# Two output blocks at a time from seven half products instead of eight, in the gate, silu and output projections of a two-layer trunk

## The chip, the core and the metric

The kernel runs on one core of a Trainium2 chip. TensorE multiplies, VectorE and ScalarE work on tiles in SBUF and PSUM, and the SyncE queue (SP in the profile) issues every transfer. The metric is the device time of one execution, in microseconds (us). A kernel is executed several times; the median of the runs is its time.

## The reference, cut to what matters

640 tokens (512 latent, 128 context) pass through two layers. Each layer normalises its input `x`, modulates it to `h` (1024 features), projects it with `w_in`, runs three mixers (attention, DeltaNet, gated MLP) and merges them:

```
h    = rms(x) * (1 + scale) + shift              # 640 x 1024
proj = h @ w_in                                  # among its columns: z_a, z_b, z_c (512 each), gl (3 x 1024)
br   = [o_a * silu(z_a), o_b * silu(z_b), o_c * silu(z_c)]
yb_n = br_n @ w_branch[n]                        # 512 -> 1024, n = 0, 1, 2
y    = sum_n sigmoid(gl_n) * yb_n                # gates
x    = x + gate * (y @ w_o)                      # 1024 -> 1024
```

The change touches the projections of `h` that give `z_a` and part of `gl`, and the product with `w_o`.

## The kernel before, in words

Activations lie transposed: a feature block is a tile of 128 partitions (features) by 640 columns (tokens), and `h` is eight such tiles. An output block is 128 output features by 640 tokens. `dense` computes one in two halves of 320 columns, each a PSUM accumulation over the eight feature blocks. To keep single precision, every operand is split into a high part (rounded to the fast 32-bit format) and a low part (the remainder), and `mm3` adds three products: high by high, high by low, low by high. So one output block takes 2 x 8 x 3 = 48 matmuls of 320 columns, two blocks 96.

A weight block of 1024 x 128 comes as two tiles of 128 x 512 in buffers tagged `raw` (three of them). `wsplit` makes `hi` by a ScalarE copy and `lo` by a VectorE subtraction (three buffers each), one pair for each 128 x 512 tile. `h` lies split in the tiles `hh0`..`hh7` and `hl0`..`hl7`, later in a layer `y` takes the same tiles.

In a layer the order of the program is: DeltaNet and MLP, attention, then `branch(2)`, `branch(1)`, `branch(0)`, then the output projection with `w_o`. In `branch(n)`, `silu_block` makes the four `z` blocks (only n = 0 and 1), which are multiplied with the mixer's output and split (tiles `qkv`). Then, for m = 0..7, a gate block comes from `h` (48 matmuls, a ScalarE tanh of each half into a `th` tile), a block of `w_branch` from the split mixer (24 matmuls), and VectorE multiplies and adds into `yacc[m]` (tile `ya`). In layer 0, `branch(0)` also runs pieces of the modulation of the next layer between its blocks (`mod_fill`, weights in `G` tiles). After the branches, `yacc` is split into `hh`/`hl`, and eight blocks of `w_o` follow; the old `x`, which each needs, comes back by a transfer into an `ld` tile. At the end of layer 0 every new `x` block is also spilled and squared for the next norm (`norm_add`).

The order of the instructions is not that of the program. All operations are recorded and then placed on the engines by a planner (`Recorder.plan`), which simulates them with estimated costs: of the operations whose inputs are ready, each engine takes the one that comes first in the program; those recorded under `rec.hp()` go before all others. Tiles of one tag get their buffers strictly in program order, so an operation can't start until all earlier tiles of its tag have had theirs. That is why blocks of the branches run already during attention (their tags are `raw`, `hi`, `lo`, `dn`), as work for TensorE between the steps of the softmax. PSUM has two buffers of one bank (`dn`), two of one bank (`mm`) and two of two banks (tag `p2`, called p in the profile), which attention uses for its scores. The numbers of buffers that matter here: `G` 13, `V` 3, `qkv` 8, `C` 5, `D` 6, `iv` 8, `raw`, `hi` and `lo` 3 each.

The loop of the output projection:

```
        for m in range(KM):
            wk = wsplit(a["w_o"][l, m, 0]) + wsplit(a["w_o"][l, m, 1])
            xo = X("ld", [P, NT])
            SY.dma_start(xo, xsrc[m])
...
            dense(wk, yh, yl, evac)
```

Of the kernel before, what the change touches and what calls it, by code (L numbers as in the profile page):

```python
# [8 lines left out]
F32R = mybir.dt.float32r  # L9
# [414 lines left out]
def trunk_kernel(ctx: ExitStack, tc: tile.TileContext, a, o, depth=DEPTH, dump=None):  # L424
# [10 lines left out]
    def T(shape, tag, dt=F32, bufs=None, pool=None):  # L435
        uid[0] += 1
        kw = {} if bufs is None else {"bufs": bufs}
        t = (pool or sb).tile(shape, dt, tag=tag, name=f"{tag}_{uid[0]}", **kw)
        return rec.tile(t, tag, pool is ps, shape, bufs or (2 if pool is lay or pool is None else 1))
# [7 lines left out]
    def p2():  # L447
        return T([P, 1024], "p2", pool=ps, bufs=2)

    def X(tag, shape, dt=F32):  # L450
        return T(shape, tag, dt, bufs=NB[tag])
# [61 lines left out]
    def wsplit(src, m=P):  # L513

        n = src.shape[1]
        w, hi, lo = wload(src), X("hi", [P, 512], F32R), X("lo", [P, 512], F32R)
        with rec.hp():
            split_w(w[:, 0:n], hi[:, 0:n], lo[:, 0:n])
        return [(hi[:, c : c + m], lo[:, c : c + m]) for c in range(0, n, m)]
# [16 lines left out]
    class Side:  # L536
# [16 lines left out]
        def finish(self, evacs):  # L553
            for (wk, m), ac, evac in zip(self.blocks, self.acc, evacs):
                with rec.hp():
                    for hf in range(2):
                        evac(ac[hf][0:m, 0:HF], hf * HF, hf * HF + HF)


    class Mod:  # L560
# [114 lines left out]
    def spill(t):  # L675
        uid[0] += 1
        d_ = dram.tile([P, NT], F32, tag=f"sp{uid[0]}", name=f"sp{uid[0]}")
        rec.tile(d_, f"sp{uid[0]}", False, [P, NT], 1)
        SY.dma_start(d_, t)
        return d_  # L680
# [18 lines left out]
    def layer(l, md, hh, hl, fill, side):  # L699
# [7 lines left out]
        def win(b, evac):  # L707
            dense(wsplit(a["w_in"][l, b, 0]) + wsplit(a["w_in"][l, b, 1]), hh, hl, evac)
# [387 lines left out]
        def silu_block(b, tag):  # L1096
            zt = X(tag, [P, NT])

            def evac(acc, c0, c1):
                th = tanh2(acc)  # L1100
                V.scalar_tensor_tensor(zt[:, c0:c1], th, 1.0, acc, ALU.add, ALU.mult)

            win(b, evac)
            return zt
# [87 lines left out]
        def mod_fill():  # L1192

            if fill:
                next(fill[0])
                left[0] = (left[0] + 1) % 4
                if left[0] == 0:
                    fill.pop(0)


        def branch(n, brs):
            bh, bl = [], []
            for q, f in enumerate(brs):
                if n == 0:
                    mod_fill()
                if n < 2:
                    u = X("ld", [P, NT])
                    SY.dma_start(u, f)
                    f = silu_block((B_ZA, B_ZB)[n] + q, "C")
                    V.tensor_tensor(f, f, u, ALU.mult)  # L1210
                hi, lo = split2(f)
                bh.append(hi)
                bl.append(lo)
            for m in range(KM):
                if n == 0:
                    mod_fill()
                ga = {}

                def ev1(acc, c0, c1):
                    ga[c0] = X("th", [P, HF])  # L1220
                    S.activation(ga[c0], acc, AF.Tanh, scale=0.5)

                win(B_GL + 8 * n + m, ev1)
                first = len(yacc) <= m
                if first:
                    yacc.append(T([P, NT], f"ya{m}", bufs=1))
                y = yacc[m]

                def ev2(acc, c0, c1):
                    if first:  # L1230
                        V.scalar_tensor_tensor(y[:, c0:c1], ga[c0], 1.0, acc, ALU.add, ALU.mult)
                    else:
                        V.scalar_tensor_tensor(ga[c0], ga[c0], 1.0, acc, ALU.add, ALU.mult)
                        V.tensor_tensor(y[:, c0:c1], y[:, c0:c1], ga[c0], ALU.add)

                dense(wsplit(a["w_branch"][l, n, m]), bh, bl, ev2)
# [273 lines left out]
        for k in range(KM):  # L1510
# [4 lines left out]
            yh.append(hi_)  # L1515
            yl.append(lo_)
        last = l == depth - 1
        for m in range(KM):
            wk = wsplit(a["w_o"][l, m, 0]) + wsplit(a["w_o"][l, m, 1])
            xo = X("ld", [P, NT])  # L1520
            SY.dma_start(xo, xsrc[m])
            xn = T([P, NT], f"ya{m}", bufs=1)

            def evac(acc, c0, c1):
                cuts = ((0, c1, 0),) if c0 == 0 else ((c0, NL, 0), (NL, c1, 1))
                for b0, b1, s in cuts:
                    V.scalar_tensor_tensor(xn[:, b0:b1], acc[:, b0 - c0 : b1 - c0], md.gate[:, m, s : s + 1], xo[:, b0:b1], ALU.mult, ALU.add)

            dense(wk, yh, yl, evac)
            if last:  # L1530
                SY.dma_start(o["y"][:, m, :], xn)
            else:
                xt[m] = xn
                xsrc[m] = spill(xn)
                sq = norm_add(m)
        return None if last else sq


# [137 lines left out]
```

## Time and profile before

| | |
|---|---|
| median of 3 runs | 1734.79 us (1727.08 to 1734.96) |
| the profiled execution | 1730.23 us, its span 1728.4 us |
| TensorE matmul busy, instructions | 1680.2 us, 13550 |
| VectorE busy, instructions | 1078.8 us, 3202 |
| ScalarE busy, instructions | 812.6 us, 2065 |
| mean granted TensorE clock | 0.991 of full speed |

The span runs from the first to the last instruction; the rest of the execution's own time, 1.8 us, lies around it. Busy time counts overlapping instructions of an engine once. Matmuls are pipelined, so their durations overlap, and the distance from start to start says what one costs in a dense row. All operations are recorded by one helper, so every row bears its line, L372, and the tiles' names tell the operations apart.

### The profile page before, as it was taken

What the parts mean: (1) busy time and instruction counts of PE and PEld (TensorE: products, weight loads), DVE (VectorE), ACT (ScalarE), POOL (GpSimd) and SP (SyncE); (2) the same over time, 40 slices, a digit from 0 to 9 for tenths busy, and PEclk for the clock granted to TensorE, in tenths of its full rate; (3) what the DMA queues carried; (4) which work ended last, traced back from release to release, by engine and by line L of the source; (5) the groups of instructions that cost most, each with busy time, mean ns of one, the idle gap of its engine ahead of it and who ended that gap; (6) DMA issues with size and microseconds to landing.
All of it is one profiled execution on the core that took longest, in us unless ns stands there. A gap on an engine that the chain in (4) does not pass through costs nothing.

```text
span 1728.4 us, 34853 instructions
## 1 busy us (share of the span) xinstructions
PE 1680.2 (97%) x13550; PEld 1574.2 (91%) x13550; DVE 1078.8 (62%) x3202; ACT 812.6 (47%) x2065; POOL 16.6 (1%) x100
## 2 busy tenths in 40 slices
PE   6999999999999999999999999899999999999999
PEld 4998988999889889999989989889989888999999
DVE  4898898565656653433568988975655666434353
ACT  3566664554545542222335666655544555423231
POOL 0000000000000000000000000000000000000000
PEclk9999999999999999999999999999999999999999
DMA  9311221221112242655432212112221122123234
GB/s 289 94 57 51 61 56 56 67 63 53 56 48 70 64 135 74 188 170 167 134 126 69 57 38 60 60 52 66 67 59 54 38 82 60 58 79 104 74 97 133
DMA packets 94612, 146.36 MB, mean 85 GB/s; under 512 B 14064, under 2 KB 38000, under 8 KB 94448
## 3 DMA queue, kind: packets, MB, share of 16 engines
q1 hardware_dynamic: 94448, 144.15, 27.6%
q8 instruction: 106, 1.74, 0.4%
q14 instruction: 58, 0.48, 0.1%
HBM read 132.28 MB, written 11.83 MB: 83 GB/s over the span
## 4 chain that ended last, share of the span: by engine, by line
PE 89%; DVE 5%; ACT 4%; issue 1%; DMA 1%; SPq 0%; DVEq 0%; ACTq 0%
PE dn L372 63%; PE p L372 14%; PE mm L372 12%; ACT iv L372 1%; DVE C L372 1%; ACT G L372 1%; DVE G L372 1%; DVE iv L372 1%; DVE lo L372 1%; ACT hi L372 1%; ACT C L372 0%; DMA ya<-in_xT 0%; DVE R L372 0%; DVE qkv L372 0%; DVE st L372 0%
## 5 line engine op out<-in xcount | busy, mean ns | idle before, releaser
L372 PE MATMUL dn<-hh,hi 128*128 128x320 f32 (+1 forms) x2176 | 687.2, 316 | 5.5 <-ACT hh L372 2.2
L372 PE MATMUL dn<-hh,lo 128*128 128x320 f32 (+1 forms) x2176 | 687.3, 316 | 0.0
L372 PE MATMUL dn<-hl,hi 128*128 128x320 f32 (+1 forms) x2176 | 686.0, 315 | 0.6 <-DVE hl L372 0.6
L372 PEld LDWEIGHTS dn<-hh,hi 128*128 128x128 f32 (+1 forms) x2176 | 409.1, 188 | 18.1 <-issue 4.8
L372 PEld LDWEIGHTS dn<-hl,hi 128*128 128x128 f32 (+1 forms) x2176 | 408.9, 188 | 4.5 <-issue 1.7
L372 PEld LDWEIGHTS dn<-hh,lo 128*128 128x128 f32 (+1 forms) x2176 | 409.2, 188 | 2.4 <-issue 0.7
L372 DVE TENSOR_TENSOR lo<-raw,hi 128x512 fp32r<-128x512 f32 (+1 forms) x322 | 221.7, 688 | 233.3 <-ACT hi L372 222.1
L372 ACT CAST hi<-raw 128x512 fp32r<-128x512 f32 (+1 forms) x322 | 199.3, 619 | 300.5 <-PE dn L372 281.7
L372 PE MATMUL dn<-qkv,hi 128*128 128x320 f32 x768 | 176.3, 313 | 0.0
L372 ACT ACTIVATE th<-dn 128x320 f32<-128x320 f32 x176 | 76.7, 436 | 129.3 <-PE dn L372 129.1
L372 PEld LDWEIGHTS dn<-qkv,hi 128*128 128x128 f32 x768 | 129.9, 189 | 1.0 <-issue 1.0
L372 PE MATMUL dn<-qkv,lo 128*128 128x320 f32 x384 | 119.6, 312 | 0.0
L372 DVE TENSOR_REDUCE mx<-p 128x1 f32<-128x640 f32 x64 | 52.7, 823 | 60.3 <-PE p L372 60.3
L372 ACT ACTIVATE V<-p,mx,scl 128x640 f32<-128x640 f32 x64 | 56.8, 887 | 66.4 <-DVE mx L372 59.2
L372 PEld LDWEIGHTS dn<-qkv,lo 128*128 128x128 f32 x384 | 72.4, 189 | 0.0
L372 DVE SCALAR_TENSOR_TENSOR th<-th,dn 128x320 f32<-128x320 f32 x96 | 46.7, 486 | 40.8 <-PE dn L372 35.7
L372 PEld LDWEIGHTS p<-iv,G 32*32 32x32 f32 (+2 forms) x608 | 35.0, 133 | 36.0 <-issue 33.8
L372 ACT COPY V<-p 128x640 f32<-128x640 f32 x64 | 44.6, 697 | 48.0 <-PE p L372 47.7
L372 PE MATMUL p<-G,G 128*128 128x512 f32 x128 | 65.8, 596 | 0.0
L372 PE MATMUL mm<-V,G 128*64 128x128 f32 (+1 forms) x672 | 60.8, 278 | 0.0
L372 DVE TENSOR_TENSOR iv<-iv,iv 128x150 f32<-128x150 f32 (+15 forms) x244 | 57.9, 238 | 1.9
L372 PEld LDWEIGHTS mm<-V,G 128*64 128x64 f32 (+1 forms) x672 | 50.2, 149 | 5.8 <-issue 5.7
(305 smaller groups left out, 2345.1 us busy)
## 6 DMA issues: line engine op xcount, KB each, us to landing
raw<-in_w_in SPq DMA_DIRECT2D x244, 256.0 KB, 2.6
G<-in_w_mod SPq DMA_DIRECT2D x96, 256.0 KB, 4.4
raw<-in_w_branch SPq DMA_DIRECT2D x48, 256.0 KB, 2.6
raw<-in_w_o SPq DMA_DIRECT2D x32, 256.0 KB, 2.6
ld<-sp SPq DMA_DIRECT2D x24, 320.0 KB, 3.2
G<-in_w_uq SPq DMA_DIRECT2D x16, 192.0 KB, 2.7
ya<-in_xT SPq DMA_DIRECT2D x8, 320.0 KB, 5.8
sp<-V SPq DMA_DIRECT2D x8, 320.0 KB, 2.2
```

The lines of the kernel that those rows point to most:

```text
L372: op.ins = getattr(getattr(nc, ENG[op.eng]), op.meth)(*op.args, **op.kw)
```

## The change

`two_blocks` computes two output blocks together. The two blocks' weights are cut along the 1024 input features into an upper and a lower half: a11, a12 for the first block and a21, a22 for the second (each one 128 x 512 tile). The input is cut the same way along features, and along its 640 columns into left and right halves: b11, b12, b21, b22. The eight products of halves are replaced by Winograd's seven, of sums of weights and sums of inputs, and the results are put together by additions:

- weights: s1 = a21 + a22, s2 = s1 - a11, a11 - a21, a12 - s2 (VectorE, 128 x 512 each), and each of the seven factors is split into high and low;
- inputs: t1 = b12 - b11, t2 = b22 - t1, t3 = b22 - b12, t4 = b21 - t2, made and split once by `half_sums`, for `h` in branch 1 and for `y` after the branches;
- results: one ScalarE copy and seven VectorE additions of 128 x 320, all of which read PSUM.

Each product is 4 feature blocks x 3 = 12 matmuls of 320 columns, so a pair takes 84 matmuls. The accumulators are the four banks of the two `p2` tiles. The sums t1, t2, t3 lie in `G` (nine tiles) and `V` (three); t4 is written over the right halves of the first four input tiles, so after that the plain input isn't whole any more. a21, a22, s1, s2 lie in `D`, the results in `iv`.

It is used for the four `z` blocks of branch 0 (two pairs), all gate blocks of branch 0 (four pairs), the gates m = 4..7 of branch 1 (two pairs), and the blocks m = 2..7 of `w_o` (three pairs), in both layers: 22 pairs in all. The other blocks stay as they were. The old `x` for the output projection is loaded into `qkv` tiles instead of `ld`.

```diff
--- before.py
+++ after.py
@@ -555,6 +555,97 @@
                 with rec.hp():
                     for hf in range(2):
                         evac(ac[hf][0:m, 0:HF], hf * HF, hf * HF + HF)
+    def half_sums(full, xh, xl):
+        L_, R_ = slice(0, HF), slice(HF, NT)
+        b, t1, t2, t3, late = [], [], [], [], []
+        for k in range(4):
+            x0, x1 = full(k), full(k + 4)
+            t = X("C", [P, NT])
+            V.tensor_tensor(t[:, L_], x0[:, R_], x0[:, L_], ALU.subtract)
+            V.tensor_tensor(t[:, R_], x1[:, R_], x0[:, R_], ALU.subtract)
+            V.tensor_tensor(x0[:, L_], x1[:, R_], t[:, L_], ALU.subtract)
+            t4 = X("iv", [P, HF])
+            V.tensor_tensor(t4, x1[:, L_], x0[:, L_], ALU.subtract)
+            hi, lo, two = X("G", [P, NT], F32R), X("V" if k < 3 else "G", [P, NT], F32R), X("G", [P, NT], F32R)
+            S.copy(hi, t)
+            V.tensor_tensor(lo, t, hi, ALU.subtract)
+            S.copy(two[:, L_], x0[:, L_])
+            V.tensor_tensor(two[:, R_], x0[:, L_], two[:, L_], ALU.subtract)
+            t1.append((hi[:, L_], lo[:, L_]))
+            t3.append((hi[:, R_], lo[:, R_]))
+            t2.append((two[:, L_], two[:, R_]))
+            late.append(t4)
+        def last():
+            for k in range(4):
+                S.copy(xh[k][:, R_], late[k])
+                V.tensor_tensor(xl[k][:, R_], late[k], xh[k][:, R_], ALU.subtract)
+            q = lambda k, c: (xh[k][:, c], xl[k][:, c])
+            return {"b11": [q(k, L_) for k in range(4)], "b21": [q(k + 4, L_) for k in range(4)], "b22": [q(k + 4, R_) for k in range(4)],
+                    "t1": t1, "t2": t2, "t3": t3, "t4": [q(k, R_) for k in range(4)]}
+        return last
+    def two_blocks(src, B, evac):
+        a11, a12 = wload(src[0]), wload(src[1])
+        a21, a22 = X("D", [P, 512]), X("D", [P, 512])
+        SY.dma_start(a21, src[2])
+        SY.dma_start(a22, src[3])
+        s1, s2 = X("D", [P, 512]), X("D", [P, 512])
+        ab, cd = p2(), p2()
+        qa_, qb_, qc_, qd_ = ab[:, 0:HF], ab[:, 512 : 512 + HF], cd[:, 0:HF], cd[:, 512 : 512 + HF]
+        def product(w, b, out):
+            hi, lo = X("hi", [P, 512], F32R), X("lo", [P, 512], F32R)
+            with rec.hp():
+                split_w(w, hi, lo)
+            for k, (bh, bl) in enumerate(B[b]):
+                c = slice(P * k, P * k + P)
+                mm3(out, hi[:, c], lo[:, c], bh, bl, k == 0, k == 3)
+        def plus(out, x, y):
+            with rec.hp():
+                V.tensor_tensor(out, x, y, ALU.add)
+        def minus(out, x, y):
+            with rec.hp():
+                V.tensor_tensor(out, x, y, ALU.subtract)
+        plus(s1, a21, a22)
+        minus(s2, s1, a11)
+        product(a11, "b11", qa_)
+        product(s2, "t2", qb_)
+        u, v, x, y = (X("iv", [P, HF]) for _ in range(4))
+        with rec.hp():
+            S.copy(u, qa_)
+        plus(v, qb_, u)
+        product(s1, "t1", qc_)
+        minus(a21, a11, a21)
+        plus(x, qc_, v)
+        product(a12, "b21", qa_)
+        plus(u, qa_, u)
+        minus(a12, a12, s2)
+        with rec.hp():
+            evac(0, u, 0, HF)
+        product(a21, "t3", qb_)
+        plus(y, qb_, x)
+        plus(v, qb_, v)
+        with rec.hp():
+            evac(1, y, HF, NT)
+        product(a22, "t4", qd_)
+        plus(v, qd_, v)
+        with rec.hp():
+            evac(1, v, 0, HF)
+        product(a12, "b22", qc_)
+        plus(x, qc_, x)
+        with rec.hp():
+            evac(0, x, HF, NT)
 
 
     class Mod:
@@ -1197,16 +1288,31 @@
                 if left[0] == 0:
                     fill.pop(0)
 
+        def h_sum(k):
+            x = X("C", [P, NT])
+            V.tensor_tensor(x, hh[k], hl[k], ALU.add)
+            return x
+        B = {}
 
         def branch(n, brs):
+            first2 = (0, 4, KM)[n]
             bh, bl = [], []
             for q, f in enumerate(brs):
                 if n == 0:
                     mod_fill()
+                if n == 0 and q % 2 == 0:
+                    zs = [X("C", [P, NT]) for _ in range(2)]
+                    def evz(i, acc, c0, c1):
+                        V.scalar_tensor_tensor(zs[i][:, c0:c1], tanh2(acc), 1.0, acc, ALU.add, ALU.mult)
+                    two_blocks([a["w_in"][l, B_ZA + q + i, half] for i in range(2) for half in range(2)], B, evz)
                 if n < 2:
                     u = X("ld", [P, NT])
                     SY.dma_start(u, f)
-                    f = silu_block((B_ZA, B_ZB)[n] + q, "C")
+                    f = silu_block(B_ZB + q, "C") if n else zs[q % 2]
                     V.tensor_tensor(f, f, u, ALU.mult)
                 hi, lo = split2(f)
                 bh.append(hi)
@@ -1214,13 +1320,26 @@
             for m in range(KM):
                 if n == 0:
                     mod_fill()
-                ga = {}
-
-                def ev1(acc, c0, c1):
-                    ga[c0] = X("th", [P, HF])
-                    S.activation(ga[c0], acc, AF.Tanh, scale=0.5)
-
-                win(B_GL + 8 * n + m, ev1)
+                if m >= first2:
+                    if m % 2 == 0:
+                        if not B:
+                            B.update(half_sums(h_sum, hh, hl)())
+                        gates = {}
+                        def ev0(i, acc, c0, c1):
+                            gates[i, c0] = acc
+                            S.activation(acc, acc, AF.Tanh, scale=0.5)
+                        two_blocks([a["w_in"][l, B_GL + 8 * n + m + i, half] for i in range(2) for half in range(2)], B, ev0)
+                    ga = {c0: gates[m % 2, c0] for c0 in (0, HF)}
+                else:
+                    ga = {}
+                    def ev1(acc, c0, c1):
+                        ga[c0] = X("th", [P, HF])
+                        S.activation(ga[c0], acc, AF.Tanh, scale=0.5)
+                    win(B_GL + 8 * n + m, ev1)
                 first = len(yacc) <= m
                 if first:
                     yacc.append(T([P, NT], f"ya{m}", bufs=1))
@@ -1515,24 +1634,41 @@
             yh.append(hi_)
             yl.append(lo_)
         last = l == depth - 1
+        sums = half_sums(lambda k: yacc[k], yh, yl)
+        wo = lambda m, half: a["w_o"][l, m, half]
         for m in range(KM):
-            wk = wsplit(a["w_o"][l, m, 0]) + wsplit(a["w_o"][l, m, 1])
-            xo = X("ld", [P, NT])
+            xo = X("qkv", [P, NT])
             SY.dma_start(xo, xsrc[m])
             xn = T([P, NT], f"ya{m}", bufs=1)
-
-            def evac(acc, c0, c1):
+            if m % 2 == 0:
+                outs = []
+            outs.append((xn, xo))
+            def evac(i, acc, c0, c1):
+                xn, xo = outs[i]
                 cuts = ((0, c1, 0),) if c0 == 0 else ((c0, NL, 0), (NL, c1, 1))
+                mi = m - m % 2 + i
                 for b0, b1, s in cuts:
-                    V.scalar_tensor_tensor(xn[:, b0:b1], acc[:, b0 - c0 : b1 - c0], md.gate[:, m, s : s + 1], xo[:, b0:b1], ALU.mult, ALU.add)
-
-            dense(wk, yh, yl, evac)
-            if last:
-                SY.dma_start(o["y"][:, m, :], xn)
+                    V.scalar_tensor_tensor(xn[:, b0:b1], acc[:, b0 - c0 : b1 - c0], md.gate[:, mi, s : s + 1], xo[:, b0:b1], ALU.mult, ALU.add)
+            if m < 2:
+                dense(wsplit(wo(m, 0)) + wsplit(wo(m, 1)), yh, yl, lambda acc, c0, c1: evac(m, acc, c0, c1))
+                done = [m]
+                if m == 1:
+                    B = sums()
+            elif m % 2 == 0:
+                continue
             else:
-                xt[m] = xn
-                xsrc[m] = spill(xn)
-                sq = norm_add(m)
+                two_blocks([wo(m - 1 + i, half) for i in range(2) for half in range(2)], B, evac)
+                done = [m - 1, m]
+            for n in done:
+                xn = outs[n % 2][0]
+                if last:
+                    SY.dma_start(o["y"][:, n, :], xn)
+                else:
+                    xt[n] = xn
+                    xsrc[n] = spill(xn)
+                    sq = norm_add(n)
         return None if last else sq
```

## Rows read from the trace of the kernel before

**Rows 1.** The page's part 1: engines, busy us, share of the span, instructions.

```profile
PE 1680.2 (97%) x13550; PEld 1574.2 (91%) x13550; DVE 1078.8 (62%) x3202; ACT 812.6 (47%) x2065; POOL 16.6 (1%) x100
```

**Rows 2.** The page's part 4, the chain that ended last, by engine.

```profile
PE 89%; DVE 5%; ACT 4%; issue 1%; DMA 1%; SPq 0%; DVEq 0%; ACTq 0%
```

**Rows 3.** Windows: us, busy PE, PEld, DVE, ACT, POOL, PEclk, DMA share, GB/s.

```profile
657.30:699.50 42.20, 42.20 (x293) 42.01 (x291) 15.79 (x28) 10.52 (x21) 0.00 (x0) 1.00 0.26 75
699.50:827.00 127.50, 127.50 (x967) 118.37 (x967) 53.20 (x108) 36.29 (x67) 0.00 (x0) 1.00 0.55 174
827.00:883.50 56.50, 56.50 (x388) 56.50 (x387) 27.52 (x51) 16.40 (x26) 0.34 (x6) 1.00 0.49 155
1513.30:1555.50 42.20, 42.20 (x290) 42.20 (x289) 15.79 (x28) 10.56 (x20) 0.00 (x0) 1.00 0.27 76
1555.50:1668.20 112.70, 112.70 (x771) 112.70 (x770) 50.36 (x85) 36.37 (x67) 0.00 (x0) 1.00 0.31 86
1668.20:1724.80 56.60, 56.45 (x385) 56.19 (x384) 21.49 (x43) 9.42 (x15) 0.00 (x0) 1.00 0.43 136
```

**Rows 4.** Timeline of PE, layer 1's first w_o matmuls: start us, us, what.

```profile
1668.17 0.31 PE L372 MATMUL dn<-hh,hi 128*128 128x320 f32 x1
...
1669.93 0.31 PE L372 MATMUL dn<-hh,hi 128*128 128x320 f32 x1
```

**Rows 5.** Groups by form: names, shapes, count | busy us, mean ns | idle before.

```profile
L372 DVE TENSOR_TENSOR lo<-raw,hi 128x512 fp32r<-128x512 f32 x320 | 220.6, 689 | 233.3 <-ACT hi L372 222.1 <-DMA G<-in_w_mod 4.1 <-PE mm L372 3.3
L372 ACT CAST hi<-raw 128x512 fp32r<-128x512 f32 x320 | 198.2, 620 | 293.7 <-PE dn L372 280.6 <-issue 7.3 <-ACT G L372 2.5
L372 DVE SCALAR_TENSOR_TENSOR th<-th,dn 128x320 f32<-128x320 f32 x96 | 46.7, 486 | 40.8 <-PE dn L372 35.7 <-ACT th L372 4.9
L372 DVE TENSOR_TENSOR ya<-ya,th 128x320 f32<-128x320 f32 x64 | 31.5, 492 | 2.0
L372 DVE SCALAR_TENSOR_TENSOR ya<-dn,gate,ld 128x320 f32<-128x320 f32 x16 | 8.8, 551 | 47.9 <-DMA ld<-in_xT 22.4 <-DMA ld<-sp 19.9 <-PE dn L372 5.6
L372 DVE TENSOR_TENSOR ya<-ya,ld 128x512 f32<-128x512 f32 x8 | 5.5, 688 | 0.1
```

**Rows 6.** Timeline of DVE around the end of branch 0, layer 0.

```profile
801.75 0.49 DVE L372 SCALAR_TENSOR_TENSOR th<-th,dn 128x320 f32<-128x320 f32 x1 [0.56 <-PE dn L372]
802.28 0.49 DVE L372 TENSOR_TENSOR ya<-ya,th 128x320 f32<-128x320 f32 x1
...
822.88 0.69 DVE L372 TENSOR_TENSOR lo<-raw,hi 128x512 fp32r<-128x512 f32 x1
823.49 1.55 DVE L372 TENSOR_TENSOR hl<-ya,hh 128x640 fp32r<-128x640 f32 x2
...
825.56 0.48 DVE L372 SCALAR_TENSOR_TENSOR th<-th,dn 128x320 f32<-128x320 f32 x1
825.96 0.82 DVE L372 TENSOR_TENSOR hl<-ya,hh 128x640 fp32r<-128x640 f32 x1
826.69 0.49 DVE L372 TENSOR_TENSOR ya<-ya,th 128x320 f32<-128x320 f32 x1
```

**Rows 7.** Timeline of DVE in layer 0's output projection.

```profile
848.37 0.68 DVE L372 SCALAR_TENSOR_TENSOR ya<-dn,gate,ld 128x192 f32<-128x192 f32 x2 [0.35 <-PE dn L372]
848.96 0.68 DVE L372 TENSOR_TENSOR lo<-raw,hi 128x512 fp32r<-128x512 f32 x1
849.85 0.83 DVE L372 TENSOR_TENSOR C<-C,C 128x640 f32<-128x640 f32 x1 [0.21 <-ACT C L372]
```

**Rows 8.** Tile V, 630 to 660 us: ns min/median/max, first and last start.

```profile
L372 PE MATMUL mm<-V,G x32: 272/273/324, 631.5 to 642.1; 128*64 128x128 f32 x32
```

**Rows 9.** Tile V, whole span: attention's last product in layer 1.

```profile
L372 PE MATMUL mm<-V,Q x128: 272/273/273, 413.2 to 1498.5; 128*64 128x128 f32 x128
```

**Rows 10.** Transfers: KB each, median us from issue to landing.

```profile
raw<-in_w_in SPq DMA_DIRECT2D x244, 256.0 KB, 2.6
G<-in_w_mod SPq DMA_DIRECT2D x96, 256.0 KB, 4.4
```

## The prediction

> **What bounds the kernel now.** I read the page's busy shares first, then the chain that ended last, then the windows around the places that change, and last single starts on TensorE and VectorE. TensorE is busy 97% of the span, VectorE 62%, ScalarE 47% [rows 1], and the chain gives 89% of the span to TensorE [rows 2]. From the end of attention to the end of a layer TensorE has no gap: its busy time equals the window in five of the six windows of [rows 3], and misses 0.15 us in the sixth, the end of the kernel. The granted clock there is 1.00, the 2.4 GHz level. VectorE is busy 37 to 49% of these windows (15.79 of 42.20, 27.52 of 56.50). So there a matmul less is time less, as long as VectorE, which pays for the saving, keeps up.
>
> **What is removed.** In a dense row a 320-column matmul starts 1.76 us after the twelfth before it [rows 4], 0.1467 us each; a window agrees, 56.45 us for 385 [rows 3]. A pair goes from 96 to 84 matmuls, 14.08 to 12.32 us, and saves 1.76 us. Eleven pairs in each of two layers: 22 x 1.76 = 38.7 us, of it 28.2 in the h pairs and 10.6 in the y pairs. The Trainium skill (TensorE: Matmul & The Clock Gate, Back-to-back issue gap) gives N/2.4 + 2.5 ns, 135.8 ns for 320 columns; by it the saving would be 35.9 us, but the trace has 146.7 ns, and I use that.
>
> **What is added on VectorE.** Price is the distance from start to start where nothing is waited for: 0.61 us for 512 columns (822.88 to 823.49), 0.40 for 320 (825.56 to 825.96), 0.73 for 640 (825.96 to 826.69) [rows 6]. A plain f32 addition of 512 takes 688 ns against 689 for the split, and an addition of 320 takes 492 against 486 for one that reads PSUM, so one price serves each size [rows 5]. The durations are 0.08 longer than these distances, and the upper bound: an operation that needs the result of the one just before it waits it out (801.75, 0.49 long, then 802.28) [rows 6]. I take the distances, since the planner has independent operations to put between, and keep the durations for the range.
>
> The Trainium skill (VectorE: DVE Perf Modes, The DRAIN you can't avoid) says that the next VectorE operation doesn't start until the pipe of the one before is empty. By it every operation would cost its full duration; the starts 0.08 us before the end of the one ahead speak against it, and it is weighed as a rival below.
>
> A pair needs seven splits and four weight sums of 512 and seven result sums of 320: 11 x 0.61 + 7 x 0.40 = 9.51 us of VectorE, where it had four splits (2.44). To this come in each place:
> - Gate pair (6 a layer): two splits for w_branch and eight operations of 320, 9.51 + 1.22 + 3.20 = 13.93 us. TensorE has 84 + 48 matmuls, 19.36 us. VectorE has 5.4 us to spare: no loss.
> - z pair (2 a layer): four operations of 320 for silu and four of 640 (product with the mixer, split), 9.51 + 1.60 + 2.92 = 14.03 us against 12.32: 1.7 us too much each. In layer 0 the modulation's matmuls stand between (967 in the window, where eight blocks of 72 and four of 48 make 768) [rows 3] and cover it. In layer 1 up to 3.4 us are lost, and part goes into the spare time of the gate pairs beside it. I take 2 (0 to 4).
> - w_o pair (3 a layer): the final operations on 320, 192 and 128 columns, about 1.07 us a block (0.55 [rows 5], and 0.68 for a pair of 192 and 128 [rows 7], less overlaps): 9.51 + 2.14 = 11.65 against 12.32 in layer 1. In layer 0 the norm's 640-column sum comes to each block (849.85) [rows 7]: 13.11. That loses 0.8 x 3 = 2.4 in layer 0; at 95% busy in layer 1 latencies show, and I take 0.5 x 3. Together 4 (2 to 8).
>
> ScalarE gains three copies of 0.62 [rows 5] and one of 320 a pair, some 2.3 us, where it is busy 17 to 32% [rows 3]: nothing.
>
> **The input sums.** For h: four times (six of 320 and one of 640), 4 x 3.13 = 12.5 us, and eight re-additions of 640, 5.8: 18.4 us of VectorE a layer. They may run once attention gives buffers back. Attention's last product starts at 642.1 in layer 0 [rows 8] and near 1498.5 in layer 1 [rows 9]; the fifth gate block, the first that needs them, begins 42.2 us (4 x 72 matmuls) ahead of branch 0, at 657.3 and 1513.3 [rows 3]. That leaves 15 us of TensorE work on block m = 3, a block like the four behind it, which keep VectorE 37% busy, and only parts that need `V` have to wait even so long. I cost them at nothing; without that cover it is up to 18.4 us a layer.
>
> For y the cover is two dense blocks, 14.08 us, and one product. In the same time VectorE must finish the last branch block (1.6), the last split of y (0.73), the sums (12.5), three splits (1.83), the two blocks' final operations (2.14) and the second product's weights (four operations, 2.44): 21.2 us against 14.08 + 1.76 = 15.84. The second product of the first pair would be 5.4 us late, with every later product queued behind it on TensorE. The first two sums need only yacc[0], [1], [4], [5], which are ready before the last gate pair's spare time; I take 3 us a layer, 6 in all (2 to 12).
>
> **Waits and moves.** PSUM: each bank comes back two or three products after its use, over 3 us, so TensorE shouldn't wait for it. xo in `qkv` instead of `ld`: its buffers come free with branch 0's last products and the block's result needs it 3.5 us later; before, VectorE already sat waiting for this transfer (22.4 and 19.9 us in all) without a gap on TensorE [rows 3, 5]. Cost nothing; if late, the results hold two accumulators and the first block stops for a few us a layer.
> `G`: the sums hold nine of 13 buffers through branch 0, so the modulation's groups of four weight tiles in layer 0 have four instead of 13. A load lands 4.4 us after issue [rows 10], and can be issued only when the group before has run. SP issues in order: behind a load that waits for a buffer stand the `raw` and `D` loads of the next pair. Twelve groups; the planner puts them apart, and I take 2 us in all (0 to 53, twelve full landings).
> Two of four weight tiles of a pair go to `D` (six, four held by a pair): loads land in 2.6 us [rows 10] and a pair lasts 12: nothing. The ends of the two layers get one addition longer on the path: 1 us.
>
> **Sum.** -38.7 + 2 + 4 + 0 + 6 + 2 + 1 = -23.7, from the profiled execution's 1730.2: 1706.5, say 1707 us. That execution lies 4.6 us under the median shown (1734.79); a measurement of this kernel can't tell much under 0.5%, some 9 us, from no change.
>
> **Rivals.**
> - All is hidden. VectorE has room in total: 22 x 7.07 + 2 x 18.4 + 2 x 12.5 = 217 us more than 1078.8, some 76% of the new span. For it: the planner may fill every gap. Against: w_o, where the sums have nothing to hide behind. Only the 1 us at the ends is left: 1692.5. Chance 0.13.
> - VectorE sets the pace, at full durations (0.69, 0.49, 0.82), as dependent operations pay and as the page above would have it for all. A pair is 11.0 us, a z pair 16.3, a w_o pair 13.6 or 15.3, the y sums 15.0. z loses 3.9 x 4, half of it covered: 8. The second w_o product is about 9 us late, 2 covered: 14 in both layers. The w_o pairs lose 1.3 x 3 + 3.0 x 3 = 12.8. With 3 for the rest: 37.8 of 38.7, 1729 us. For it: the chains s1 to s2, t1 to t2, and sums that follow products. Against: the starts in [rows 6]. Chance 0.17, of which 0.05 is for an end low enough to be faster by over 0.5%.
> - Slower: the modulation's loads in layer 0 stop the SP queue. Each group then shows its landing of 4.4 us to TensorE, 53 us instead of 2: 1757. It turns the gain into a loss from 2.1 us a group on (25.7 / 12), and into one over 0.5% from 2.9. For it: four buffers instead of 13 and an in-order queue. Against: only layer 0 has these loads, and a gate pair's 19.36 us hold two groups. Chance 0.08.
> - The forecast, 1698 to 1717: chance 0.62.
>
> The likeliest is faster: 0.62 + 0.13 + 0.05 = 0.80; same 0.12; slower 0.08. The range that leaves out no more than 2 in 10 reaches from all hidden to VectorE's pace, 1691 to 1728.
>
> **What would show it.** 264 matmuls fewer, about 13286. TensorE without gaps in the second half of branch 1 (38.7 instead of 42.2 us) and nearly so in branch 0 (10.6 us shorter); a gap of some 3 us in w_o after two dense blocks, ended by VectorE's `C`, `G` or `V`; w_o about as long as before (56.5), so that nearly all gain lies in the h pairs. VectorE's busy time near 1300 us, above 85% in w_o, with starts 0.40 and 0.61 apart.
> Wrong would make it: VectorE at durations in these rows; gaps at the first gate pair, which I take as covered; TensorE waiting for `raw`, `D` or `G` transfers; or a planner's order that changes the rest of the kernel, where nothing was changed, by more than a few us.

## The result, and the profile after

The changed kernel takes 1754.90 us (median of 4 runs, 1751.78 to 1754.97), the kernel before 1731.89 beside it (1727.08 to 1734.96): a ratio of 1.0134 [1.0114, 1.0153]. It is 1.3% slower; the forecast, 1707 us, was 23.7 us (1.4%) faster than the execution that it starts from (1730.2). The profiled execution took 1754.95 us, its span 1753.2.

Page of the changed kernel, part 1 (engines, busy us, share of the span, instructions) and the chain that ended last, by engine:

```profile
PE 1664.7 (95%) x13286; PEld 1539.1 (88%) x13286; DVE 1294.2 (74%) x3638; ACT 888.9 (51%) x2201; POOL 16.6 (1%) x100
...
PE 44%; DVE 4%; ACT 3%; issue 1%; DVEq 0%; ACTq 0%
```

The work is what the prediction counted: 264 matmuls fewer than in [rows 1], and VectorE at 1294 us (1300 forecast). But TensorE's share has fallen from 97% to 95%, though its work fell too: it now waits somewhere. Its busy time understates that, since matmuls overlap and a pause of under 1 us is partly covered by the modelled end of the one ahead.

The same six stretches as [rows 3], in the changed kernel: second half of branch 1, branch 0 and output projection, first in layer 0, then in layer 1 (us, busy PE, PEld, DVE, ACT, POOL, granted clock, DMA share, GB/s):

```profile
655.81:700.58 44.77, 41.41 (x283) 39.05 (x281) 31.66 (x58) 16.43 (x29) 0.00 (x0) 1.00 0.23 71
700.58:831.96 131.38, 121.29 (x883) 107.81 (x880) 98.42 (x197) 51.54 (x91) 0.00 (x0) 1.00 0.50 159
831.96:896.24 64.28, 59.68 (x415) 53.24 (x413) 56.32 (x114) 27.57 (x49) 0.17 (x3) 1.00 0.59 200
1529.47:1573.15 43.68, 40.32 (x267) 38.73 (x265) 30.79 (x56) 15.81 (x28) 0.00 (x0) 1.00 0.25 73
1573.15:1689.36 116.21, 106.63 (x699) 102.15 (x697) 94.64 (x174) 52.18 (x92) 0.00 (x0) 1.00 0.26 79
1689.36:1748.70 59.34, 53.69 (x350) 50.96 (x348) 50.50 (x103) 21.32 (x38) 0.00 (x0) 1.00 0.34 119
```

Every stretch is longer than its counterpart in [rows 3], five of the six with fewer matmuls (the third now holds 64 of the next layer's modulation), all at the full 2.4 GHz level. Branch 0 of layer 1 has 72 matmuls fewer and takes 116.21 us instead of 112.70. VectorE isn't full there (94.64 of 116.21), nor in the second half of branch 1 (30.79 of 43.68), where TensorE misses 3.36 us all the same. The waits view of TensorE in the first two stretches of layer 1, 1529.4 to 1689.4, has two rows (waiting engine and tile, releaser, us in all, times, longest us):

```profile
PE p L372 <- DVE iv L372: 9.3, 16, 0.6
PE p L372 <- ACT iv L372: 3.6, 7, 0.5
```

Before, TensorE had nothing to wait for there: busy time and window agree in [rows 3]. All waits now are those of `p`, the accumulators of `two_blocks`, for an operation that writes `iv`, that is, for the additions (DVE) and the copy (ACT) that read a product. Layer 1's branches have eight pairs: 16 and 7 waits, so two for an addition and one for the copy in each pair, except one pair that has none for the copy.

### The profile page after: what moved, and what is told of

Read it like the earlier page. It is cut to its first block, busy times and chain, and to the rows that moved or that the text cites. A ratio compares the mean times of both kernels' runs of the same rounds, so it can differ in the third digit from the quotient of the medians.

```text
span 1753.2 us, 34923 instructions
## 1 busy us (share of the span) xinstructions
PE 1664.7 (95%) x13286; PEld 1539.1 (88%) x13286; DVE 1294.2 (74%) x3638; ACT 888.9 (51%) x2201; POOL 16.6 (1%) x100
## 4 chain that ended last, share of the span: by engine, by line
PE 44%; DVE 4%; ACT 3%; issue 1%; DVEq 0%; ACTq 0%
PE dn L372 21%; PE p L372 17%; PE mm L372 6%; DVE iv L372 1%; ACT iv L372 1%; ACT G L372 1%; DVE G L372 0%; ACT hi L372 0%; DVE C L372 0%; DVE lo L372 0%; DVE R L372 0%; ACT C L372 0%; ACT V L372 0%; ACT th L372 0%; ACT Q L372 0%
## 5 line engine op out<-in xcount | busy, mean ns | idle before, releaser
L372 PE MATMUL dn<-hh,hi 128*128 128x320 f32 (+1 forms) x1472 | 470.1, 320 | 7.4 <-ACT hh L372 4.1
L372 PE MATMUL dn<-hh,lo 128*128 128x320 f32 (+1 forms) x1472 | 470.0, 319 | 0.0
L372 PE MATMUL dn<-hl,hi 128*128 128x320 f32 (+1 forms) x1472 | 468.9, 319 | 0.0
L372 PEld LDWEIGHTS dn<-hh,hi 128*128 128x128 f32 (+1 forms) x1472 | 277.3, 188 | 15.9 <-ACT hh L372 5.5
L372 PEld LDWEIGHTS dn<-hl,hi 128*128 128x128 f32 (+1 forms) x1472 | 277.4, 189 | 4.1 <-issue 2.0
L372 PEld LDWEIGHTS dn<-hh,lo 128*128 128x128 f32 (+1 forms) x1472 | 277.5, 189 | 2.5 <-issue 0.7
L372 PE MATMUL p<-hh,hi 128*128 128x320 f32 x384 | 121.3, 317 | 11.1 <-DVE iv L372 10.5
L372 PE MATMUL p<-G,hi 128*128 128x320 f32 x396 | 103.9, 319 | 20.2 <-ACT iv L372 10.3
L372 PE MATMUL p<-hh,lo 128*128 128x320 f32 x384 | 119.5, 311 | 1.8 <-DVE iv L372 1.8
L372 PE MATMUL p<-hl,hi 128*128 128x320 f32 x384 | 118.8, 310 | 0.6 <-DVE iv L372 0.6
```

Source lines behind the costliest of these rows:

```text
L372: op.ins = getattr(getattr(nc, ENG[op.eng]), op.meth)(*op.args, **op.kw)
```

## One pair in the trace

The places within a pair show the cause. The timeline of TensorE in the first pair of layer 1 (start us, us, engine, line, operation, tiles, [idle before <- releaser]); matmuls start 0.147 us apart, except at three places (and 0.25 us behind the first matmul after each):

```profile
1531.96 0.31 PE L372 MATMUL p<-G,lo 128*128 128x320 f32 x1
1532.78 0.56 PE L372 MATMUL p<-G,hi 128*128 128x320 f32 x2 [0.52 <-ACT iv L372]
...
1537.15 0.31 PE L372 MATMUL p<-hh,lo 128*128 128x320 f32 x1
1537.29 0.30 PE L372 MATMUL p<-G,hi 128*128 128x320 f32 x1
1537.44 0.31 PE L372 MATMUL p<-V,hi 128*128 128x320 f32 x1
1537.59 0.31 PE L372 MATMUL p<-G,lo 128*128 128x320 f32 x1
1538.48 0.41 PE L372 MATMUL p<-G,hi 128*128 128x320 f32 x1 [0.58 <-DVE iv L372]
```

The timelines of VectorE and ScalarE in the same pair:

```profile
1537.93 0.49 DVE L372 TENSOR_TENSOR iv<-p,iv 128x320 f32<-128x320 f32 x1 [1.00 <-PE p L372]
1538.34 0.68 DVE L372 TENSOR_TENSOR lo<-raw,hi 128x512 fp32r<-128x512 f32 x1
```

```profile
1532.30 0.43 ACT L372 COPY iv<-p 128x320 f32<-128x320 f32 x1 [0.40 <-PE p L372]
```

Product 4 ends with the matmul of 1537.15 (to 1537.46). Its result is in the first bank of tile `ab`, and VectorE is idle, but the addition that reads it starts at 1537.93 only. Product 5 has begun at 1537.29, in the *second* bank of the same tile; its third matmul ends at 1537.90, and the addition starts just behind it. Then product 5's fourth matmul, which needs nothing new of its own, waits until the addition is over (1538.42) and starts at 1538.48, 0.89 us behind the third. So reading one bank and writing the other exclude each other in both directions, though no number is shared.

That wait is in the program. In the changed kernel's list of TensorE instructions, the last gate pair of layer 1 has it at these places, in the middle of products, where no operand is new (the product and the matmul's place in it, tile names with their numbers, and the engine whose semaphore is waited for):

```
product 2,  6th: p2_4228_4296<-G_3951_4019,lo_4233_4301
product 2,  7th: p2_4228_4296<-G_3958_4026,hi_4232_4300 [waits Activation]
...
product 5,  3rd: p2_4228_4296<-G_3942_4010,lo_4243_4311 [waits DVE]
product 5,  4th: p2_4228_4296<-G_3949_4017,hi_4242_4310 [waits DVE]
...
product 7,  6th: p2_4229_4297<-hh5_2332_2400,lo_4247_4315
product 7,  7th: p2_4229_4297<-hh6_2335_2403,hi_4246_4314 [waits DVE]
```

The wait of product 5's third matmul is for the split `lo` of the new weights. Those of the 7th, the 4th and the 7th are for the copy and the two additions that read the other bank of the tile, and each of these three in turn waits for the matmul just ahead. The planner's own record of what depends on what tells banks apart (its `box` makes a mask of 512-column banks for a PSUM tile), so it placed the reads between the next product's matmuls as free. The waits that were put in behind it tell only tiles apart. It happens wherever consecutive products share a tile: `ab` to `ab` behind product 1 and behind product 4, `cd` to `cd` behind product 6. Three pauses of 0.82 to 0.89 us from start to start, 0.67 to 0.74 beyond the normal 0.147; 63 of the 66 places show it; in two the modulation's matmuls of layer 0 fill the pause, and one pair has none behind product 1. The second matmul after a pause lies about 0.1 us later still (0.25 behind the first in place of 0.147), so a pause costs some 0.8 us, and 63 of them some 50 us, against 38.7 saved.

The theories, then. **One:** this wait by tiles. **Two:** VectorE sets the pace, which 74% busy and a next start after 0.41 us (1537.93 to 1538.34) speak against, but the pauses do end with a VectorE addition. **Three:** the chip itself can't read one PSUM bank while TensorE writes the neighbouring one. By one, the tile that each accumulator lies in alone decides; by two that changes nothing; by three, neighbouring banks in different tiles pause too.

## The experiments

**Alternating accumulators (`alt`).** The same products in the same order, but each consecutive pair lies in different tiles.

```diff
-        qa_, qb_, qc_, qd_ = ab[:, 0:HF], ab[:, 512 : 512 + HF], cd[:, 0:HF], cd[:, 512 : 512 + HF]
+        qa_, qc_, qb_, qd_ = ab[:, 0:HF], ab[:, 512 : 512 + HF], cd[:, 0:HF], cd[:, 512 : 512 + HF]
...
-        product(a12, "b21", qa_)
+        product(a12, "b21", qd_)
...
-        product(a21, "t3", qb_)
+        product(a21, "t3", qa_)
...
-        product(a22, "t4", qd_)
+        product(a22, "t4", qb_)
```

> All 22 pairs as in the changed kernel, but consecutive products go into different two-bank tiles: ab, cd, ab, cd, ab, cd, ab instead of ab, ab, cd, ab, ab, cd, cd. Theory 1 (a matmul into one bank of a two-bank tile waits for the read of the other bank of that tile): the three pauses of 0.82 to 0.89 us in each pair go, 0.73 us each beyond a normal start and some 0.1 for the restart, 66 x 0.8 = 53 us: about 1702 us. Theory 2 (VectorE's added work sets the pace): TensorE still waits as long in all, about 1755. Theory 3 (reading PSUM on VectorE while TensorE writes PSUM costs on the chip itself): reads and writes still coincide, about 1755.

Measured: 1702.54 us (1701.18 to 1704.85) against 1730.66 before, ratio 0.9835 [0.9818, 0.9853]. The change of tiles alone is worth 52 us. Its page, part 1, and the six stretches (columns as above):

```profile
PE 1643.2 (97%) x13286; PEld 1535.7 (90%) x13286; DVE 1289.8 (76%) x3638; ACT 885.0 (52%) x2201; POOL 16.6 (1%) x100
```

```profile
653.94:693.75 39.81, 39.81 (x282) 39.03 (x280) 31.55 (x58) 16.23 (x29) 0.00 (x0) 1.00 0.25 80
693.75:810.46 116.71, 116.71 (x883) 107.73 (x879) 97.21 (x197) 50.74 (x91) 0.00 (x0) 1.00 0.57 179
810.46:870.14 59.68, 56.91 (x414) 52.97 (x412) 56.48 (x115) 27.87 (x50) 0.17 (x3) 1.00 0.63 217
1500.46:1539.19 38.73, 38.73 (x267) 38.73 (x266) 30.64 (x56) 15.61 (x28) 0.00 (x0) 1.00 0.27 83
1539.19:1641.48 102.29, 102.29 (x698) 102.10 (x697) 92.78 (x174) 51.46 (x92) 0.00 (x0) 1.00 0.31 90
1641.48:1694.90 53.42, 52.09 (x350) 50.98 (x348) 49.92 (x103) 21.04 (x38) 0.00 (x0) 1.00 0.37 131
```

TensorE is without a gap again through both branches. Four such pauses are left in the output projections (three in layer 0, 1.8 us in the waits view, and one in layer 1), where VectorE reads so late that the next product but one, in the same tile again, has begun. The read behind product 4 now starts while product 5 goes on (timelines of VectorE and of TensorE, layer 1's first pair):

```profile
1507.71 0.49 DVE L372 TENSOR_TENSOR iv<-p,iv 128x320 f32<-128x320 f32 x1 [0.56 <-PE p L372]
...
1511.72 0.69 DVE L372 TENSOR_TENSOR D<-D,raw 128x512 f32<-128x512 f32 x1
1512.33 0.68 DVE L372 TENSOR_TENSOR lo<-raw,hi 128x512 fp32r<-128x512 f32 x1
```

```profile
1507.36 0.31 PE L372 MATMUL p<-hh,lo 128*128 128x320 f32 x1
...
1507.80 0.31 PE L372 MATMUL p<-G,lo 128*128 128x320 f32 x1
1507.95 0.30 PE L372 MATMUL p<-G,hi 128*128 128x320 f32 x1
```

The addition begins 0.04 us after product 4's last matmul ends (1507.67) instead of 0.47, and the matmuls keep their 0.147 through it. Theory two falls: the same VectorE work, in 52 us less.

**Four tiles (`sep`).** Theory three could still hold of the two banks of a tile alone. Here the products keep the order of the changed kernel, and each accumulator has a tile of its own: two of the single banks that the dense blocks use, and one bank of each two-bank tile.

```diff
-        ab, cd = p2(), p2()
-        qa_, qb_, qc_, qd_ = ab[:, 0:HF], ab[:, 512 : 512 + HF], cd[:, 0:HF], cd[:, 512 : 512 + HF]
+        qa_, qb_, qc_, qd_ = (t[:, 0:HF] for t in (pdense(), pdense(), p2(), p2()))
```

> The changed kernel with its own order of accumulators, but each of the four in a tile of its own: the first two in the one-bank tiles of the dense blocks, the other two in one half each of a two-bank tile. Reads and writes coincide as in the changed kernel. Theory 1 (the wait is on the shared tile): no pauses of 0.82 to 0.89 us inside the pairs, a time near the alternating one, 1703 us; some us more are possible where a pair and a dense block now share their tiles. If it were the order of products and reads or the PSUM itself: 1755, as the changed kernel.

Measured: 1701.70 us (1700.62 to 1704.52) against 1729.36, ratio 0.9842 [0.9827, 0.9858]. The pauses are gone, whether or not consecutive products lie in different kinds of tile. Tiles decide, not the order. The program as built gives the two one-bank tiles the banks 6 and 7, which are neighbours, so products 4 and 5 are the case of theory three: one bank read while the next is written, in different tiles. Timelines of VectorE and of TensorE in layer 1's first pair, where the pause stood in the changed kernel:

```profile
1511.37 0.49 DVE L372 TENSOR_TENSOR iv<-dn,iv 128x320 f32<-128x320 f32 x1 [0.56 <-PE dn L372]
```

```profile
1511.46 0.31 PE L372 MATMUL dn<-G,lo 128*128 128x320 f32 x1
1511.61 0.31 PE L372 MATMUL dn<-G,hi 128*128 128x320 f32 x1
1511.75 0.31 PE L372 MATMUL dn<-V,hi 128*128 128x320 f32 x1
```

The addition runs from 1511.37 to 1511.86, and the matmuls into the neighbouring bank keep their 0.147 us. Theory three falls for these neighbours.

**The wait in the old kernel (`wo_shared`).** The kernel before, with the two halves of a `w_o` block in the two banks of one tile in place of two tiles; nothing else of it changes.

```diff
-            dense(wk, yh, yl, evac)
+            two = p2()
+            for hf in range(2):
+                acc = two[:, 512 * hf : 512 * hf + HF]
+                cs = slice(hf * HF, hf * HF + HF)
+                for k, (wh, wl) in enumerate(wk):
+                    mm3(acc, wh, wl, yh[k][:, cs], yl[k][:, cs], k == 0, k == len(wk) - 1)
+                with rec.hp():
+                    evac(acc, hf * HF, hf * HF + HF)
```

> The kernel before, where only the output projection's two halves of a block lie in the two banks of one tile instead of two tiles: no work added or removed. Theory 1: in each of the 16 blocks the second half's matmuls wait once for VectorE's read of the first half, 0.7 to 0.9 us: 11 to 14 us slower than before, about 1743. Otherwise no change, 1731.

Measured: 1744.76 us (1743.75 to 1746.69) against 1729.36, ratio 1.0090 [1.0075, 1.0106]: 15.4 us for 16 blocks, 0.96 a block. That is a little more than expected. The timeline of TensorE shows the one pause of a block, 0.95 us from start to start; in the program it stands behind the tenth matmul of the second half in all 16 blocks, and the read of the first half waits for that matmul. The waits view for layer 1's projection counts eight, where the kernel before has no row:

```profile
1681.17 0.30 PE L372 MATMUL p<-hh,hi 128*128 128x320 f32 x1
1682.12 0.41 PE L372 MATMUL p<-hl,hi 128*128 128x320 f32 x1 [0.64 <-DVE ya L372]
```

```profile
PE p L372 <- DVE ya L372: 5.2, 8, 0.7
```

No sums of halves and no added VectorE work are in this kernel, so the wait needs neither. Theory one is shown by removal twice and by insertion once. The program of the kernel before and that of `sep` have no wait of one bank for the other bank of its tile; this one has 16.

**Parts of the change.** With the pauses out, what is each half of the change worth? `h_only` is the changed kernel's pairs on `h`, with the output projection of before; `alt_h` is the same with alternating tiles; `alt_y` has the pairs on `y` alone, alternating; `alt_last` is `alt` with pairs on `y` in layer 1 only. The edit of the first two is the loop of the output projection put back:

```diff
-        sums = half_sums(lambda k: yacc[k], yh, yl)
...
+            wk = wsplit(a["w_o"][l, m, 0]) + wsplit(a["w_o"][l, m, 1])
+            xo = X("ld", [P, NT])
...
+            dense(wk, yh, yl, evac)
```

> The 16 pairs on h as in the changed kernel, the output projection as before. Against before: 16 x 1.76 = 28 us saved and 48 pauses of 0.8 us added, 38 us, so by theory 1 about 1732 + 10 = 1742 and the same three pauses in each pair. By theory 2 about as much, since the pauses are there whatever makes them; what is left to 1755 is the price of the y pairs: 13.

> The 16 pairs on h with alternating tiles, the output projection as before. Theory 1: 28 us saved, a few lost in the z pairs: about 1706. Theories 2 and 3: as the run with the h pairs alone, 1742.

> The six pairs on y with alternating tiles, the branches as before. Theory 1: 10.6 us saved, less the late sums (3 us a layer), the norm in layer 0 (4) and the end of layer 0 (TensorE stood 5.5 us there in the changed kernel, against 2.7 before): between 1728 and 1735, no change. Theory 2: the output projection is the one stage where VectorE has more work than TensorE, so 1740 or more.

> Alternating tiles, the pairs on y in layer 1 alone; layer 0's output projection as before. The trace of the alternating kernel has TensorE idle for 1.2, 2.5 and 2.6 us where layer 0 ends, with the granted clock at 0.50 behind it, against 1.0 to 1.5 at the full clock where layer 0's projection is dense. If y's pairs lose all they save there: 1699 us, 3 to 4 below the run with the pairs on h alone and with those on both. If they pay in both layers, 1705.

| kernel | us, median | ratio to before |
|---|---|---|
| `h_only` | 1740.23 (1738.98 to 1741.59) | 1.0052 [1.0035, 1.0069] |
| `alt_h` | 1702.78 (1699.84 to 1704.03) | 0.9833 [0.9815, 0.9851] |
| `alt_y` | 1735.08 (1730.23 to 1736.80) | 1.0015 [0.9999, 1.0032] |
| `alt_last` | 1700.46 (1698.01 to 1704.39) | 0.9832 [0.9816, 0.9848] |

`h_only` minus `alt_h` is 37.4 us for 16 pairs, 0.78 a pause with three pauses each. `alt_h` alone has all the gain: 27.9 us under the 1730.66 beside it, where 16 x 1.76 = 28.2 are saved on paper. The pairs on `y` bring nothing that can be measured; they save 10.6 on paper. Where that goes is read from `alt` against `alt_h`, whose output projections are (windows of `alt_h`, layer 0 and 1):

```profile
813.56:869.88 56.32, 56.32 (x387) 56.32 (x386) 26.89 (x49) 16.37 (x25) 0.34 (x6) 1.00 0.50 157
1641.94:1698.20 56.26, 56.26 (x386) 56.22 (x384) 21.13 (x42) 9.46 (x15) 0.00 (x0) 1.00 0.42 134
```

In layer 1 `alt` takes 53.42 us against 56.26: 2.8 gained of 5.3. In layer 0 it takes 59.68 against 56.32, but 64 matmuls of the next layer's modulation (4.5 us busy) lie inside this window in `alt` and behind it in `alt_h` (5.1 us). There they cover the chain of the next norm; in `alt` that cover is gone, and TensorE stands still twice. Timeline of TensorE and two windows at the end of layer 0 in `alt`:

```profile
870.14 2.39 PE L372 MATMUL p<-c_ones,C 128*128 128x1 f32 x20 [0.95 <-DVE C L372]
...
875.17 2.50 PE L372 MATMUL p<-c_ident,R 128*128 128x128 f32 x10 [2.36 <-DVE R L372]
880.00 0.50 PE L372 MATMUL dn<-hh,hi 128*48 128x320 f32 x1 [2.32 <-ACT hh L372]
```

```profile
875.00:880.00 5.00, 2.51 (x11) 2.22 (x11) 1.68 (x4) 1.47 (x3) 0.00 (x0) 0.50 0.01 2
880.00:885.00 5.00, 5.00 (x23) 4.52 (x24) 5.00 (x12) 3.01 (x6) 0.00 (x0) 0.63 0.00 0
```

From the start of the projection to the first matmul of the next layer (880.00) `alt` takes 69.5 us; `alt_h`, which reaches it at 880.88, takes 67.3. So 5.3 us of matmuls less end 2.2 us later: 7.5 us lost in layer 0 (1.8 of it in the three pauses that `alt` keeps there) and 2.4 in layer 1, together 9.9 of 10.6.

**VectorE's room (`alt_load`).** How near is VectorE to setting the pace? `alt` with six more additions of 320 columns in each pair, into `th` tiles that nothing reads: 132 x 0.40 = 53 us of VectorE whose sums are not used.

```diff
+        for _ in range(6):
+            plus(X("th", [P, HF]), s1[:, 0:HF], s2[:, 0:HF])
         product(a11, "b11", qa_)
```

> Alternating tiles and six more VectorE additions of 128 x 320 in every pair, whose results nobody reads: 2.4 us a pair, 53 us in all. If VectorE has the room that the prices from start to start give it, the 12 gate pairs (5.4 us spare) hide theirs, the four z pairs and six w_o pairs, which have none, pay up to 2.4 us each: 1703 plus 10 to 24. If VectorE set the pace throughout: 1703 + 53 = 1756.

Measured: 1735.90 us (1735.12 to 1737.18), ratio 1.0038 [1.0024, 1.0053]: 33 us over `alt`, more than I expected. By stretches of layer 1 (columns as above):

```profile
1514.77:1553.49 38.72, 38.72 (x266) 38.72 (x265) 35.18 (x72) 15.63 (x28) 0.00 (x0) 1.00 0.24 76
1553.49:1666.20 112.71, 106.41 (x698) 103.48 (x697) 104.75 (x205) 51.15 (x92) 0.00 (x0) 0.98 0.28 84
1666.20:1728.80 62.60, 54.99 (x350) 52.54 (x348) 57.08 (x121) 20.77 (x38) 0.00 (x0) 0.97 0.33 112
```

The gate pairs of branch 1, 79% busy on VectorE in `alt` (30.64 of 38.73), take 4.8 us more without a trace in the time. Branch 0 loses 10.4 us and the projection 9.2, for 14.4 and 7.2 added. But branch 0 isn't one stage. Its first part (the two z pairs, the first gate pair and some of the second) has three pairs in a row with no `w_branch` block between; the rest is gate pairs and `w_branch` blocks. The two parts with as many matmuls each in `alt`, then in `alt_load`:

```profile
1539.19:1586.91 47.72, 47.72 (x327) 47.53 (x325) 45.75 (x87) 24.89 (x45) 0.00 (x0) 1.00 0.33 99
1586.91:1641.48 54.57, 54.57 (x374) 54.57 (x373) 47.03 (x89) 26.57 (x47) 0.00 (x0) 1.00 0.28 83
```

```profile
1553.49:1611.62 58.13, 51.83 (x326) 48.90 (x325) 52.79 (x102) 25.25 (x46) 0.00 (x0) 0.97 0.29 85
1611.62:1666.20 54.58, 54.58 (x374) 54.58 (x373) 51.96 (x105) 25.91 (x46) 0.00 (x0) 1.00 0.28 83
```

All 10.4 us are lost in the first part, where VectorE was 96% busy already; in the second, at 86%, it does 4.9 us more at no cost. What tells the places apart is whether the added work still fits. VectorE's busy time with it is 35.18 us in the 38.73 that branch 1 took in `alt`, and 51.96 in the 54.57 of the second part; but it is 52.79 in the 47.72 of the first part, and 57.08 in the 53.42 of the projection. There 5.1 and 3.7 us don't fit, and 10.4 and 9.2 are lost. The places are about those that I expected; the price is higher. How much of it is the granted clock (0.97 in both) and how much the planner's order, this run doesn't tell.

## Why the prediction was wrong

Its sign was wrong by one step, in "Waits and moves": "PSUM: each bank comes back two or three products after its use, over 3 us, so TensorE shouldn't wait for it." The step asked when a bank is written again, and for that it is right. It didn't ask what else the tile of that bank is doing, and took the four banks for four buffers, when the program's waits know two tiles. It was costed at nothing and measured 52 us (the changed kernel's 1754.90 against `alt`'s 1702.54). No rival had it, and the range ended at 1728.

With that one cause out, `alt` measures the rest of the sum: 1702.5 us for 1706.5 forecast.

- What is removed: 38.7 us. In the stretches of `alt` with nothing else between, two gate pairs take 38.73 us and four dense blocks took 42.20: 3.47 for 3.52.
- z pairs (2) and modulation loads (2): nearly nothing is left of them, since `alt_h` gains 27.9 of 28.2. The rival in which the loads stop SP's queue did not occur: in `alt`, branch 0 of layer 0 shrinks by 10.8 us and TensorE has no gap in it.
- Input sums for `h`: costed at nothing, and the first gate pair starts without a gap in both layers.
- `w_o` pairs (4), sums for `y` (6), ends of the layers (1): 11 forecast, 9.9 measured, but in other places. The gap of some 3 us after the two dense blocks isn't there: in layer 0 these take 14.29 us up to the first product, and 96 matmuls are 14.08. What the sums were over-priced, the end of layer 0 was under-priced: idle stretches of 2.36 and 2.32 us and half a clock, where 1 us stood. That the two sums come out so near is luck.
- VectorE's prices: the distances from start to start. In `alt` they hold where something independent follows (1511.72 to 1512.33, 0.61), and the busy time came out within 1% of the 1300 forecast. The prediction took the Trainium skill (VectorE: DVE Perf Modes, The DRAIN you can't avoid) to have every operation wait out the one ahead; the same section adds that a next operation that isn't held starts earlier, and the trace agrees with that: 0.61 us from start to start for a duration of 0.69. Still, VectorE's pace as a rival was closer than its 0.17 said: 2.4 us more a pair, and all the gain is gone (`alt_load`).

What would have found it before the run: each accumulator's tile and bank written beside the order of the products, and the question which instructions touch the *tile* between a product's last matmul and its read. No row of the trace before shows two banks of one tile in such use by `dense`, whose halves have tiles of their own.

What stays open: whether pairs on `y` in layer 1 alone gain their 2 to 3 us. `alt_last` has the lowest median, but it was measured beside another set of the kernel before (1729.36, not 1730.66), and as ratios (0.9832, 0.9835 for `alt`, 0.9833 for `alt_h`) the three can't be told apart.

## What to carry to other kernels

Accumulators that are read while TensorE goes on with the next product belong in different tiles, not in two banks of one; list consecutive products with their tiles before costing a saving in matmuls. Where a scheduler of one's own tells more apart than the layer that puts in the waits, its plan looks free and the program waits: compare the two at the places where a plan puts a read between writes. Price added work by the part of a stage that it falls into, and ask whether it fits there: where VectorE stood at 79% and 86% it took some 5 us more at no cost, where it stood at 93% and 96% it didn't, and neither the 76% of the span nor the 91% of all of branch 0 tells them apart.

## What the hardware showed that was not expected

At the end of layer 0 TensorE's granted clock falls from 1.00 to 0.50, the 1.2 GHz level, in `alt` and in the changed kernel, and matmuls then start 0.27 us apart instead of 0.147 (in `alt` up to 883.5). The two idle stretches there, 2.36 and 2.32 us, come too late to be the whole cause. In the changed kernel the clock falls at about 898.4, while TensorE runs 20 matmuls of one column; the first idle stretch begins behind them. Timeline and windows of the changed kernel:

```profile
896.24 2.48 PE L372 MATMUL p<-c_ones,C 128*128 128x1 f32 x20
898.58 0.67 PE L372 MATMUL mm<-c_ident,mrow 128*128 128x128 f32 x2
```

```profile
898.00:898.50 0.50, 0.50 (x6) 0.50 (x6) 0.39 (x2) 0.00 (x0) 0.00 (x0) 0.91 0.54 131
898.50:899.00 0.50, 0.50 (x4) 0.34 (x3) 0.17 (x1) 0.00 (x0) 0.17 (x3) 0.50 1.04 401
```

In `alt` it falls behind the same 20 matmuls, 0.6 us into the first idle stretch. In `alt_h`, where modulation matmuls stand between the first ten and the last ten of them and the idle stretches are 0.5 to 1.1 us, it stays at 1.00. Which of these decides, no run here separates. The pauses of 0.7 us, three in a pair, did not lower it in the branches or the projections: the six stretches of the changed kernel all stand at 1.00.
